# Writing the two parts of each input-projection weight tile to DRAM once and reading them back for three later chunks

## The chip, the cores and the metric

The kernel runs on one core of one Trainium2 chip. The metric is the device time of one launch in microseconds (us). The engines are named as the profile names them: PE is TensorE's matmul, PEld its load of weights, DVE is VectorE, ACT ScalarE, POOL GpSimd, and SP the engine that issues most of the DMAs. Each engine works through its own queue of instructions in a fixed order.

## The reference

One layer of a hybrid decoder over 2048 tokens of width 1024. What matters here is that `h @ w_in` is one projection from 1024 to 3592 columns, over all tokens.

```
h   = rmsnorm(x, norm_mix) * (1.0 + sc_a) + sh_a          # (1, 2048, 1024)
proj = h @ w_in                                           # w_in: (1024, 3592)
sb_q, sb_k, sb_v, dn_qkv, dn_z, dn_a, dn_b = split(proj)  # 512 512 512 1536 512 4 4
o_a = stick_breaking_attention(rmsnorm(sb_q), rmsnorm(sb_k), sb_v)       # 8 heads x 64
q, k, v = split(silu(causal_conv(dn_qkv)))
o_b = rmsnorm(chunk_gated_delta_rule(l2norm(q), l2norm(k), v, g, beta)) * silu(dn_z)   # 4 x 128
x = x + g_a * (concat[o_a, o_b] @ w_out)
h = rmsnorm(x, norm_mlp) * (1.0 + sc_m) + sh_m
x = x + g_m * (square(relu(h @ w_ff1)) @ w_ff2)           # 1024 -> 4096 -> 1024
```

All data are f32. `sc_a`, `sh_a`, `g_a` and the three of the second half come from `silu(c) @ w_ada`.

## The kernel before

**Tiling.** The sequence is cut in four chunks of 512 tokens, which are projected in the order c = 3, 2, 1, 0. For each chunk `project` multiplies all of `w_in` with the chunk's normed activations: 24 blocks of 128 columns (k, v, q of the delta heads, then K, Q of the attention, V, and z) and a small block for the gates. So every weight is used four times, once in each chunk, and each time it is loaded from DRAM anew.

**Two parts.** A product of f32 matrices is made of three products of a shorter type, F32R: the weight tile `ws` is split into `wh`, the value rounded to F32R, and `wl`, the rest; the activations are split in the same way. TensorE adds `wh·ah`, `wh·al` and `wl·ah` (L192 to L194 in `dense`, L212 to L215 in `dense_tok`, L359 to L361 in `wide`).

**One weight unit.** `wunit` makes one pair: the load of `ws` on SP's queue (L171, 128x512 f32, 262144 bytes), the rounding on ScalarE (L172), the subtraction (L173). Of five subtractions in a row two go to GpSimd and three to VectorE. `ws`, `wh` and `wl` each have three buffers in the pool `wp`. A load into `ws` so waits for the cast and the subtraction three units earlier, and the cast for the matmuls that read the `wh` three units earlier: a load can stand six units ahead of the matmuls. A chunk has 56 units: 48 in `dense` (24 blocks, two halves of the depth each; in chunk 3 the first ten of them in `wide`, some with buffers borrowed from other tags) and 8 in `dense_tok` (V). In all there are 224.

**The rest of the mixer.** Between a chunk's projection matmuls, TensorE also does the attention (`attention`, lines L477 to L524) and the delta rule of the chunk before, in two halves of its heads (`delta_half`): pg (the product of the keys), vt and qt (transposes), M and X (a solve by steps on VectorE, L765 and L768, 58 steps for one half), paq, a recurrence, and an output norm whose result goes to DRAM (`mix_d`) and comes back as `mx` and `hm` for the output projection (`outs`, tiles mmo, weights who and wlo, also from `wunit`). The output projection of chunk 3 runs in chunk 1's turn, those of 2, 1 and 0 at the end. Each chunk has a branch (`attention_far`, L540 to L593), which every engine passes and whose body is skipped in this run: work whose instructions stand behind it can't start ahead of it. In chunk 2's turn 32 tiles of `w_ada` of 512 KB are loaded on SP's queue as well (L963, two buffers). After the mixer comes the feed-forward, which the change leaves as it is.

**The order.** The order of each engine's queue is set when the kernel is built, by a scheduler that plays through the program with estimated times and priorities. An edit in one place can so move instructions elsewhere.

Of the kernel before, what the change touches and what calls it, by code (L numbers as in the profile page):

```python
# [7 lines left out]
F32 = mybir.dt.float32  # L8
F32R = mybir.dt.float32r
# [7 lines left out]
P = 128  # L17
# [3 lines left out]
CH = 512  # L21
NCH = SEQ // CH
# [34 lines left out]
def tile_hybrid_layer(  # L57
# [17 lines left out]
    nc = tc.nc  # L75
    V, G, A, T = nc.vector, nc.gpsimd, nc.scalar, nc.tensor

    cp = ctx.enter_context(tc.tile_pool(name="cp", bufs=1))
    dr = ctx.enter_context(tc.tile_pool(name="dr", bufs=1, space=DRAM))

    mx, pms, inner, right = [ctx.enter_context(ExitStack()) for _ in range(4)]
    wp = mx.enter_context(tc.tile_pool(name="wp", bufs=3))
# [49 lines left out]
    if True:  # L132
# [28 lines left out]
        nw = [0]  # L161

        def wunit(src, name, shape=(P, 512), after=None, spots=(None,) * 3):

            ws, wh, wl = [(spot[0] if spot else wp).tile(list(shape), F32 if n == "ws" else F32R, name=n + name,
                                                         tag=spot[1] if spot else n, bufs=spot[2] if spot else 3)
                          for n, spot in zip(("ws", "wh", "wl"), spots)]
            nw[0] += 1
            with tc.high_priority():
                with tc.issue_after(after) if after is not None else nullcontext():  # L170
                    nc.sync.dma_start(ws, src)  # L171
                A.copy(wh, ws)  # L172
                (G if nw[0] % 5 < 2 else V).tensor_tensor(wl, ws, wh.bitcast(F32), ALU.subtract)  # L173
            return wh, wl

        late = []

        def run_late():
# [2 lines left out]
            for f in todo:  # L181
                f()

        def dense(acts, w, evac, name, m0=0):

            for m in range(m0, 4):
                ps = pm.tile([P, CH], F32, tag="mm", name=f"mm{name}_{m}")
                for k in range(KT):
                    if k % 4 == 0:
                        wh, wl = wunit(w[m, :, k:k + 4, :], f"{name}_{m}{k}", (P, 4, P))  # L190
                    ah, al = acts[k]
                    T.matmul(ps, lhsT=wh[:, k % 4, :], rhs=ah, start=k == 0, stop=False)  # L192
                    T.matmul(ps, lhsT=wh[:, k % 4, :], rhs=al, start=False, stop=False)
                    T.matmul(ps, lhsT=wl[:, k % 4, :], rhs=ah, start=False, stop=k == KT - 1)  # L194
                run_late()
                with tc.high_priority():
                    evac(m, ps)

        def dense_tok(acts, w, dst, name):

            for f in range(2):
                if f:
                    run_late()
                ps = [pm.tile([P, 2, 256], F32, tag="mm", name=f"mm{name}_{f}{i}") for i in range(2)]
                for k in range(KT):
                    if k % 2 == 0:
                        src = w[f, :, k:k + 2, :]
                        wh, wl = wunit(src, f"{name}_{f}{k}", (P, 2, 256))
                    ah, al = acts[k]
                    for m in range(4):  # L210
                        o, t = ps[m // 2][:, m % 2, :], slice(m * P, (m + 1) * P)
                        T.matmul(o, lhsT=ah[:, t], rhs=wh[:, k % 2, :], start=k == 0 and m % 2 == 0, stop=False,  # L212
                                 skip_group_check=True)
                        T.matmul(o, lhsT=ah[:, t], rhs=wl[:, k % 2, :], start=False, stop=False, skip_group_check=True)
                        T.matmul(o, lhsT=al[:, t], rhs=wh[:, k % 2, :], start=False, stop=k == KT - 1,  # L215
                                 skip_group_check=True)
                with tc.high_priority():
                    for i in range(2):
                        e = ev.tile([P, 2, 256], F32, tag="ev", name=f"ev{name}_{f}{i}", bufs=3)
                        A.copy(e, ps[i])  # L220
                        nc.scalar.dma_start(dst.rearrange("(m p) f -> p m f", p=P)[:, 2 * i:2 * i + 2,
                                          f * 256:(f + 1) * 256], e)
# [86 lines left out]
        def project(c, acts):  # L309
# [32 lines left out]
            def wide(acts):  # L342

                ps = [pm.tile([P, CH], F32, tag="mm", name=f"mmk{c}_{m}") for m in range(3)]
                ps += [bank(f"mmk{c}_3", [P, CH], "a"), bank(f"mmv{c}_0", [P, CH], "a")]
                spots = {(3, 0): ((at, "ald", 2), (at, "sp", 2), (at, "sp", 2)),
                         (4, 0): ((at, "ald", 2), (at, "aT0", 1), (at, "aT1", 1)),
                         (0, 4): (None, (dn, "ktok0", 1), (dn, "ktok1", 1)),
                         (1, 4): (None, (dn, "dd0", 1), (dn, "dd1", 1)),
                         (2, 4): (None, (dn, "wq0", 1), (at, "qf", 2)),  # L350
                         (3, 4): ((at, "rkb", 1), (at, "av", 2), (at, "av", 2)),
                         (4, 4): ((at, "sn", 1), (at, "om", 1), (at, "qf", 2))}
                for k0 in (0, 4):
                    ws = [wunit(w_m[12 + m, :, k0:k0 + 4, :], f"{'k' if m < 4 else 'v'}{c}_{m % 4}{k0}", (P, 4, P),
                                gate[f"dma{8 + k0}"], spots.get((m, k0), (None,) * 3)) for m in range(5)]
                    for k in range(k0, k0 + 4):
                        ah, al = acts[k]
                        for p, (wh, wl) in zip(ps, ws):
                            T.matmul(p, lhsT=wh[:, k - k0, :], rhs=ah, start=k == 0, stop=False)  # L359
                            T.matmul(p, lhsT=wh[:, k - k0, :], rhs=al, start=False, stop=False)  # L360
                            gate["pe"] = T.matmul(p, lhsT=wl[:, k - k0, :], rhs=ah, start=False, stop=k == KT - 1).ins  # L361
                with tc.high_priority():
                    for m, p in enumerate(ps):
                        conv_out(0 if m < 4 else 8)(m % 4, p)
# [35 lines left out]
            if c == NCH - 1:  # L400
                wide(acts)
            else:
                dense(acts, w_m[12:16], conv_out(0), f"k{c}")
            rs = norm_stats(c - 1) if c > 0 else None
            psab = pm.tile([64, CH], F32, tag="mm", name=f"psab{c}")
            for k in range(KT):
# [14 lines left out]
                    V.tensor_copy(abT[c], pt)  # L421
            late.append(ab_out)

            dense(acts, w_m[16:20], conv_out(8), f"v{c}", 1 if c == NCH - 1 else 0)
            dense(acts, w_m[8:12], conv_out(4), f"q{c}")
            dense(acts, w_m[4:8], head_out(kf_d, 1), f"K{c}")
            dense(acts, w_m[0:4], head_out(qf_d, 0), f"Q{c}")
            late.append(head_rstd)
            dense_tok(acts, w_v, v_d[c], f"V{c}")
            run_late()  # L430
            dense(acts, w_m[20:24], z_out, f"z{c}")
            return rs


# [546 lines left out]
        acts = []  # L981
# [317 lines left out]
```

## Time and profile before

| | us |
|---|---|
| median of 3 runs | 2868.04 |
| lowest and highest run | 2867.67, 2877.46 |
| the profiled execution | 2871.72 |
| its span in the trace | 2869.9 |
| PE busy in it | 2644.2 |
| DVE, ACT, POOL busy in it | 1874.9, 1241.4, 761.6 |

The profile is one execution of the program; the times of its instructions add up to its own time, which lies 3.68 us above the median. The span is the time from the first to the last instruction in the trace. "Busy" of an engine is the time in which it has an instruction under way. The granted clock is the part of TensorE's full clock (2.4 GHz) that it was given; between 1.2 and 2.4 GHz it changes by stages, and a mean of 0.91 is a mixture of the two.

In time, the projection of chunk 3 takes about 39 to 265 us, chunk 2's turn about 265 to 575, chunk 1's 575 to 870, the output projection of chunk 3 870 to 935, chunk 0's turn 935 to 1225, the rest of the mixer to 1510, and the feed-forward to the end.

### The profile page before, as it was taken

How to read it: one execution, taken by the hardware profiler on the slowest of the kernel's cores; microseconds unless marked ns; L12 is line 12 of the kernel's file. 1: busy time of each engine (PE TensorE's matmuls, PEld its weight loads, DVE VectorE, ACT ScalarE, POOL GpSimd, SP SyncE). 2: the span in 40 equal slices, each digit the busy share in tenths (PEclk: the TensorE clock that was granted, in tenths of full speed). 3: DMA queues.
4: the chain of work that ended last, by engine and by line, in shares of the span. 5: the costliest groups of instructions: out<-in, count | busy, mean ns of one | idle time of the engine just before them, and what ended most of it. 6: DMA issues, size and time to landing. Idle time of an engine off the chain costs nothing. (4 is left out here: it accounts for less than half of the span.)

```text
span 2869.9 us, 37558 instructions
## 1 busy us (share of the span) xinstructions
PE 2644.2 (92%) x13044; PEld 2139.5 (75%) x13044; DVE 1874.9 (65%) x4391; ACT 1241.4 (43%) x2421; POOL 761.6 (27%) x592
## 2 busy tenths in 40 slices
PE   3997789889989999899768999999998999999999
PEld 2786568767877778777646888888876888888887
DVE  7665994688748794757765655556568556555655
ACT  4553454355525464354344433343345443344332
POOL 4222311232123221213253222222235222222221
PEclk9999979999989999999989999999999999999999
DMA  7453764443436434463343111111125111111012
GB/s 249 143 165 111 227 218 151 130 139 98 147 109 204 133 120 127 131 203 126 103 137 120 59 55 34 59 59 41 48 88 176 59 59 40 50 59 59 30 59 88
DMA packets 178769, 316.79 MB, mean 110 GB/s; under 512 B 17464, under 2 KB 64504, under 8 KB 174456
## 3 DMA queue, kind: packets, MB, share of 16 engines
q1 hardware_dynamic: 168440, 299.43, 32.2%
q10 hardware_dynamic: 10112, 14.68, 1.4%
q8 instruction: 110, 1.80, 0.3%
q14 instruction: 107, 0.88, 0.1%
HBM read 258.90 MB, written 55.15 MB: 109 GB/s over the span
## 5 line engine op out<-in xcount | busy, mean ns | idle before, releaser
L1190 DVE SCALAR_TENSOR_TENSOR y<-f,mods,y 128x512 f32<-128x512 f32 x512 | 363.6, 746 | 248.2 <-PE f L1187 248.0
L1185 PE MATMUL f<-hidh,wh 128*128 128x512 f32 x1024 | 399.7, 392 | 6.4 <-DVE y L1190 6.2
L1186 PE MATMUL f<-hidl,wh 128*128 128x512 f32 x1024 | 400.4, 391 | 3.2 <-POOL hidl L1168 3.2
L1187 PE MATMUL f<-hidh,wl 128*128 128x512 f32 x1024 | 380.1, 390 | 0.8 <-POOL wl L173 0.8
L1126 PE MATMUL f<-bh,swh 128*128 128x512 f32 x896 | 355.3, 397 | 18.1 <-ACT swh L1119 18.1
L1127 PE MATMUL f<-bl,swh 128*128 128x512 f32 x896 | 354.1, 395 | 0.0
L1128 PE MATMUL f<-bh,swl 128*128 128x512 f32 x896 | 348.5, 396 | 0.7 <-DVE swl L1120 0.6
L1185 PEld LDWEIGHTS f<-hidh,wh 128*128 128x128 f32 x1024 | 192.6, 188 | 53.2 <-DVE y L1190 10.8
L1186 PEld LDWEIGHTS f<-hidl,wh 128*128 128x128 f32 x1024 | 192.7, 188 | 44.6 <-POOL hidl L1168 4.3
L1187 PEld LDWEIGHTS f<-hidh,wl 128*128 128x128 f32 x1024 | 192.6, 188 | 42.5 <-POOL wl L173 1.2
L1126 PEld LDWEIGHTS f<-bh,swh 128*128 128x128 f32 x896 | 168.4, 188 | 61.0 <-ACT swh L1119 20.4
L172 ACT CAST wh<-ws 128x512 fp32r<-128x512 f32 x128 | 79.5, 621 | 299.9 <-PE f L1186 243.6
L1128 PEld LDWEIGHTS f<-bh,swl 128*128 128x128 f32 x896 | 168.1, 188 | 43.8 <-DVE swl L1120 2.8
L1127 PEld LDWEIGHTS f<-bl,swh 128*128 128x128 f32 x896 | 168.4, 188 | 40.9 <-issue 0.2
L1168 POOL TENSOR_TENSOR hidl<-t,hidh 128x512 fp32r<-128x512 f32 x64 | 102.1, 1595 | 335.0 <-ACT hidh L1167 315.4
L1119 ACT CAST swh<-wa 128x512 fp32r<-128x512 f32 x96 | 59.4, 622 | 265.5 <-PE f L1127 259.2
L1112 POOL TENSOR_TENSOR sws<-wa 128x512 f32<-128x512 f32 x64 | 88.9, 1389 | 309.6 <-DVE wl L173 284.8
L1140 DVE TENSOR_TENSOR t<-t,f 128x512 f32<-128x512 f32 x128 | 87.3, 683 | 121.0 <-PE f L1128 87.3
L1120 DVE TENSOR_TENSOR swl<-sws,swh 128x512 fp32r<-128x512 f32 x128 | 143.1, 1118 | 22.2 <-ACT swh L1119 22.2
L1120 DVE TENSOR_TENSOR swl<-wa,swh 128x512 fp32r<-128x512 f32 x96 | 86.8, 907 | 100.2 <-ACT swh L1119 100.2
L173 POOL TENSOR_TENSOR wl<-ws,wh 128x512 fp32r<-128x512 f32 x52 | 68.1, 1311 | 247.5 <-ACT wh L172 247.0
L1141 ACT ACTIVATE t<-t 128x512 f32<-128x512 f32 x128 | 80.8, 632 | 86.2 <-DVE t L1140 86.2
(353 smaller groups left out, 6193.0 us busy)
## 6 DMA issues: line engine op xcount, KB each, us to landing
wa<-in_w_ff_dram SPq DMA_DIRECT2D x32, 1024.0 KB
ws<-in_w_ff_dram SPq DMA_DIRECT2D x128, 256.0 KB
wada<-in_w_ada_dram SPq DMA_DIRECT2D x48, 512.0 KB
wso<-in_w_out_dram SPq DMA_DIRECT2D x64, 256.0 KB
cv_d<-ev SPq DMA_DIRECT2D x48, 256.0 KB
cv<-cv_d SPq DMA_DIRECT2D x24, 512.0 KB
x<-in_xc_dram SPq DMA_DIRECT2D x40, 256.0 KB
wsk<-in_w_m_dram SPq DMA_DIRECT2D x32, 256.0 KB
```

The source lines that it names most:

```text
L1112: G.tensor_tensor(t, x, y, op)
L1120: V.tensor_tensor(wl, x, wh.bitcast(F32), SUB)
L1126: T.matmul(ps, lhsT=wh[:, k, :], rhs=ah, start=first and k == 0, stop=False, skip_group_check=True)
L1127: T.matmul(ps, lhsT=wh[:, k, :], rhs=al, start=False, stop=False, skip_group_check=True)
L1128: T.matmul(ps, lhsT=wl[:, k, :], rhs=ah, start=False, stop=stop and k == 3, skip_group_check=True)
L1140: V.tensor_tensor(t, t, ps, op)
L1141: A.activation(t, t, AF.Relu)
L1168: (G if i % 2 else V).tensor_tensor(hl, x, hh.bitcast(F32), SUB)
L1185: T.matmul(ps[n], lhsT=wh[:, s], rhs=ah, start=j == 0, stop=False)
L1186: T.matmul(ps[n], lhsT=wh[:, s], rhs=al, start=False, stop=False)
L1187: T.matmul(ps[n], lhsT=wl[:, s], rhs=ah, start=False, stop=j == 1)
L1190: V.scalar_tensor_tensor(ys[m][:, cs], ps[n], mods[:, 40 + m:41 + m], ys[m][:, cs], ALU.mult, ALU.add)
```

## The change

A new function `wparts` takes the place of `wunit` for the 56 units of the input projection. For chunk 3, which is projected first, it calls `wunit` as before and then writes `wh` (on ScalarE's queue) and `wl` (on SP's queue) to DRAM tiles, 112 writes of 262144 bytes. For the chunks 2, 1 and 0 there is no load of `ws`, no cast and no subtraction: `wh` and `wl` are loaded, both on SP's queue, 336 loads where 168 were. For every third unit the two tiles take the buffers of the tag `ws`, so that the buffers of all three tags stay in use. The output projection and the feed-forward still use `wunit`, whose counter `nw` goes on counting.

```
...
+        wm_d = [[dr.tile([2, P, CH], F32, name=f"wm_d{m}_{k}") for k in range(2)] for m in range(24)]
+        wv_d = [[dr.tile([2, P, CH], F32, name=f"wv_d{f}_{k}") for k in range(4)] for f in range(2)]
+
+        def wparts(c, src, dst, name, shape, after=None, spots=(None,) * 3):
+            if c < NCH - 1:
+
+                nw[0] += 1
+                ws = [wp.tile(list(shape), F32R, name=n + name, tag="ws" if nw[0] % 3 == 0 else n, bufs=3)
+                      for n in ("wh", "wl")]
+                with tc.high_priority():
+                    for i, t in enumerate(ws):
+                        nc.sync.dma_start(t.bitcast(F32), dst[i].rearrange("p (a b) -> p a b", a=shape[1]))
+                return ws
+            ws = wunit(src, name, shape, after, spots)
+            for i, t in enumerate(ws):
+                (nc.sync if i else nc.scalar).dma_start(dst[i].rearrange("p (a b) -> p a b", a=shape[1]), t.bitcast(F32))
+            return ws
...
-                        wh, wl = wunit(w[m, :, k:k + 4, :], f"{name}_{m}{k}", (P, 4, P))
+                        src, shape = w[m, :, k:k + 4, :], (P, 4, P)
+                        if parts is None:
+                            wh, wl = wunit(src, f"{name}_{m}{k}", shape)
+                        else:
+                            c, m_in = parts
+                            wh, wl = wparts(c, src, wm_d[m_in + m][k // 4], f"{name}_{m}{k}", shape)
...
-                        wh, wl = wunit(src, f"{name}_{f}{k}", (P, 2, 256))
+                        wh, wl = wparts(c, src, wv_d[f][k // 2], f"{name}_{f}{k}", (P, 2, 256))
...
-                    ws = [wunit(w_m[12 + m, :, k0:k0 + 4, :], f"{'k' if m < 4 else 'v'}{c}_{m % 4}{k0}", (P, 4, P),
+                    ws = [wparts(c, w_m[12 + m, :, k0:k0 + 4, :], wm_d[12 + m][k0 // 4],
+                                 f"{'k' if m < 4 else 'v'}{c}_{m % 4}{k0}", (P, 4, P),
...
```

The other lines of the diff hand `(c, m_in)` or `c` to `dense` and `dense_tok`. In the code after, the loads are line L188, the writes L192; the casts and subtractions keep L172 and L173, and later lines move down by 24 or 25.

**Where the order moves.** On SP in the projection of chunk 3, at the loads for the q blocks (`ws`, L171) and the columns that go to DRAM for the convolution (`cv_d`), the order of before is:

```order
L171 DMA wsq3_00_842<-in_w_m_dram 128x512
L333 DMA cv_d3_102<-ev3_8_619 128x512
L171 DMA wsq3_04_860<-in_w_m_dram 128x512
L333 DMA cv_d3_102<-ev3_9_737 128x512
L171 DMA wsq3_10_888<-in_w_m_dram 128x512
L171 DMA wsq3_14_906<-in_w_m_dram 128x512
L171 DMA wsq3_20_934<-in_w_m_dram 128x512
L333 DMA cv_d3_102<-ev3_10_786 128x512
L171 DMA wsq3_24_952<-in_w_m_dram 128x512
```

The order of after at the same place, with the writes to wm_d (L192):

```order
L171 DMA wsq3_10_980<-in_w_m_dram 128x512
L192 DMA wm_d19_1_189<-wlv3_34_902 128x512
L171 DMA wsq3_14_1000<-in_w_m_dram 128x512
L192 DMA wm_d8_0_166<-wlq3_00_932 128x512
L171 DMA wsq3_20_1030<-in_w_m_dram 128x512
L192 DMA wm_d8_1_167<-wlq3_04_952 128x512
L357 DMA cv_d3_102<-ev3_10_870 128x512
L171 DMA wsq3_24_1050<-in_w_m_dram 128x512
L192 DMA wm_d9_0_168<-wlq3_10_982 128x512
L171 DMA wsq3_30_1080<-in_w_m_dram 128x512
L192 DMA wm_d9_1_169<-wlq3_14_1002 128x512
```

Each load of a `ws` is now followed by the write of a `wl` of a unit four or so earlier.

On SP in chunk 2's turn, at the loads for the v and q blocks among those of `w_ada` (wada), before:

```order
L333 DMA cv_d2_101<-ev2_3_4072 128x512
L171 DMA wsv2_30_4299<-in_w_m_dram 128x512
L689 DMA cv2_1_0_5483<-cv_d2_101 128x4x256
L963 DMA wada25_9419<-in_w_ada_dram 128x1024
L171 DMA wsv2_34_4317<-in_w_m_dram 128x512
L963 DMA wada26_9423<-in_w_ada_dram 128x1024
L171 DMA wsq2_00_4346<-in_w_m_dram 128x512
L963 DMA wada27_9427<-in_w_ada_dram 128x1024
L459 DMA akf3_3_3349<-kf_d3_90 128x512
```

And after:

```order
L988 DMA wada24_9471<-in_w_ada_dram 128x1024
L188 DMA whv2_24_4412<-wm_d18_1_187 128x512
L188 DMA wlv2_24_4413<-wm_d18_1_187 128x512
L714 DMA cv2_1_0_5539<-cv_d2_101 128x4x256
L988 DMA wada25_9475<-in_w_ada_dram 128x1024
L188 DMA wlv2_20_4397<-wm_d18_0_186 128x512
L188 DMA whv2_34_4455<-wm_d19_1_189 128x512
L988 DMA wada26_9479<-in_w_ada_dram 128x1024
L988 DMA wada27_9483<-in_w_ada_dram 128x1024
L188 DMA whv2_30_4439<-wm_d19_0_188 128x512
L188 DMA wlv2_30_4440<-wm_d19_0_188 128x512
```

A unit's one load became two, `wh` and `wl`; of a unit in the tag `ws` (here v2_20) the second load stands apart from the first, behind loads of later units.

On PE at the last branch, that of chunk 0: pg is the product of the keys of half 0 of the delta heads, mmo1 the output projection of chunk 1. Before, the first rows behind the branch (the jump is its end) are:

```order
L542 UNCONDITIONAL_BRANCH x2
L192 MATMUL mmo1_0_3_27694<-hm1_1_27522,who1_0_30_27696 128x512
L193 MATMUL mmo1_0_3_27694<-lm1_1_27523,who1_0_30_27696 128x512
L194 MATMUL mmo1_0_3_27694<-hm1_1_27522,wlo1_0_30_27697 128x512
L192 MATMUL mmo1_0_3_27694<-hm1_2_27528,who1_0_30_27696 128x512
L731 MATMUL pg0_0_1_19551<-cv0_0_0_19497 128x128 x4
L193 MATMUL mmo1_0_3_27694<-lm1_2_27529,who1_0_30_27696 128x512
```

After, ahead of the branch, between the attention's matmuls of chunk 0 (z, pa):

```order
L756 MATMUL pg0_0_0_19396<-cv0_0_0_19329 128x128 x4
L502 MATMUL z0_3_11_20244<-maskr_145,identr_144 128x2x128
L509 MATMUL z0_3_11_20244<-akf0_3_20181,qf0_3_20188 128x256 x2
L260 MATMUL ss22_27190<-idon_69,acc22_26836 128x1 x4
L720 MATMUL vt0_0_1_19415<-idon_69,cv0_0_8_19409 128x128 x4
L720 MATMUL vt0_0_0_19421<-idon_69,cv0_0_8_19409 128x128 x4
L538 MATMUL pa0_3_1_0_20267<-idon_69,sp0_3_1_20242 128x128 x4
L538 MATMUL pa0_3_1_1_20274<-idon_69,sp0_3_1_20242 128x128 x4
L720 MATMUL qt0_0_1_19569<-idon_69,cv0_0_4_19562 128x128 x4
```

The products pg and the transposes vt and qt of half 0 moved from behind the last branch to ahead of it. On VectorE 16 of the 58 steps X of this half moved ahead of it with them (none stood there before), and on PE 54 matmuls of mmo1 moved from ahead of the branch to behind it: 171 stand there after, 117 before.

## Rows read from the trace of the kernel before

**Rows 1.** The page's parts 1 and 5: PE over the span, one feed-forward matmul group.

```profile
PE 2644.2 (92%) x13044; PEld 2139.5 (75%) x13044; DVE 1874.9 (65%) x4391; ACT 1241.4 (43%) x2421; POOL 761.6 (27%) x592
...
L1185 PE MATMUL f<-hidh,wh 128*128 128x512 f32 x1024 | 399.7, 392 | 6.4 <-DVE y L1190 6.2
```

**Rows 2.** Stretches: bounds, length, busy PE, PEld, DVE, ACT, POOL (instructions), clock, DMA, GB/s.

```profile
39.00:265.00 226.00, 198.25 (x1086) 165.95 (x1086) 145.43 (x455) 106.04 (x210) 57.27 (x50) 0.95 0.47 154
265.00:575.00 310.00, 270.19 (x1449) 216.79 (x1448) 239.63 (x781) 141.87 (x311) 75.66 (x64) 0.91 0.56 179
575.00:870.00 295.00, 268.41 (x1585) 221.13 (x1584) 207.77 (x661) 139.59 (x317) 64.66 (x61) 0.94 0.40 125
935.00:1225.00 290.00, 271.84 (x1576) 221.90 (x1576) 210.69 (x685) 143.03 (x325) 59.96 (x54) 0.95 0.42 128
...
1510.00:2870.00 1360.00, 1338.56 (x5770) 1081.56 (x5770) 801.47 (x1055) 530.71 (x892) 375.01 (x263) 0.99 0.19 65
```

**Rows 3.** PE's waits, 265 to 1225 us: total, times, longest.

```profile
PE pa L513 <- DVE nt L125: 11.1, 1, 11.1
...
PE mmz L192 <- ACT whz L172: 1.1, 1, 1.1
```

**Rows 4.** Stretch view, the middle of chunk 2's turn, columns as in rows 2.

```profile
300.00:450.00 150.00, 122.58 (x541) 92.38 (x540) 143.60 (x468) 78.03 (x164) 24.91 (x19) 0.85 0.68 221
```

**Rows 5.** Stretch view of line L173 alone: bounds, length, busy DVE, POOL, clock, DMA.

```profile
265.00:575.00 310.00, 25.73 (x36) 32.92 (x23) 0.91 0.56 179
575.00:870.00 295.00, 23.44 (x33) 29.00 (x22) 0.94 0.40 125
935.00:1225.00 290.00, 24.04 (x34) 29.79 (x23) 0.95 0.42 128
300.00:450.00 150.00, 11.68 (x16) 15.92 (x10) 0.85 0.68 221
```

**Rows 6.** DVE's timeline: start, length, instruction.

```profile
308.24 1.52 DVE L173 TENSOR_TENSOR wlk<-wsk,whk 128x512 fp32r<-128x512 f32 x1
...
322.48 0.69 DVE L173 TENSOR_TENSOR wlv<-wsv,whv 128x512 fp32r<-128x512 f32 x1
```

**Rows 7.** Line L173, 265 to 1225 us: shortest, median, longest ns, first and last start.

```profile
L173 DVE TENSOR_TENSOR wlk<-wsk,whk x15: 676/683/1518, 266.4 to 977.4; 128x512 fp32r<-128x512 f32 x15
...
L173 DVE TENSOR_TENSOR wlq<-wsq,whq x14: 646/681/693, 385.0 to 1057.7; 128x512 fp32r<-128x512 f32 x14
...
L173 POOL TENSOR_TENSOR wlq<-wsq,whq x10: 1270/1291/2257, 393.0 to 1046.7; 128x512 fp32r<-128x512 f32 x10
```

**Rows 8.** Stretch view of single slices, columns as in rows 2.

```profile
10.00:20.00 10.00, 1.70 (x8) 1.71 (x8) 7.63 (x16) 6.43 (x11) 0.18 (x1) 1.00 1.01 362
320.00:330.00 10.00, 9.26 (x48) 6.16 (x45) 10.00 (x33) 5.91 (x18) 0.00 (x0) 1.00 0.90 299
```

**Rows 9.** Timelines of the queues of SP and ACT: DMA issues.

```profile
325.25 11.68 SPq L963 DMA_DIRECT2D wada<-in_w_ada_dram  x4
...
145.69 0.34 ACTq L373 DMA_DIRECT2D kf_d<-ev  x1
```

**Rows 10.** ACT's timeline: casts after a late load, idle time and its end in brackets.

```profile
161.65 0.62 ACT L172 CAST whQ<-wsQ 128x512 fp32r<-128x512 f32 x1 [4.71 <-DMA wsQ<-in_w_m_dram]
...
555.43 0.62 ACT L172 CAST whz<-wsz 128x512 fp32r<-128x512 f32 x1 [9.85 <-DMA wsz<-in_w_m_dram]
```

**Rows 11.** Stretch view, from the last branch to the last mix, columns as in rows 2.

```profile
1350.00:1454.00 104.00, 75.18 (x437) 61.33 (x436) 73.35 (x287) 29.67 (x72) 29.94 (x26) 0.88 0.33 104
```

**Rows 12.** DVE's timeline behind the last branch.

```profile
1353.74 0.69 DVE L871 TENSOR_REDUCE so<-sqo 128x4 f32<-128x512 f32 x1 [3.84 <-ACT who L172]
...
1369.48 1.25 DVE L751 STREAM_TRANSPOSE M<-Gt 128x1024 f32<-128x1024 f32 x1 [0.94 <-POOL Gt L737]
```

**Rows 13.** Line L768, 1350 to 1510 us, the solve's steps.

```profile
L768 DVE TENSOR_TENSOR X<-X,tm x58: 157/183/1328, 1372.1 to 1405.0; 128x24 f32<-128x24 f32 x6, 128x27 f32<-128x27 f32 x4, 128x30 f32<-128x30 f32 x4, 128x26 f32<-128x26 f32 x3
```

**Rows 14.** ACT's timeline at the end of the mixer.

```profile
1452.01 1.89 ACT L892 CAST hm<-mx 128x512 fp32r<-128x512 f32 x3 [10.34 <-DMA mx<-mix_d]
```

More of the change, by code (lines that the diff above doesn't have):

```diff
@@ L182, in run_late, with dense @@
                 f()
-        def dense(acts, w, evac, name, m0=0):
+        def dense(acts, w, evac, name, m0=0, parts=None):
             for m in range(m0, 4):
@@ L197, in dense, with dense_tok @@
                     evac(m, ps)
-        def dense_tok(acts, w, dst, name):
+        def dense_tok(acts, w, dst, name, c):
             for f in range(2):
@@ L402, in project @@
             else:
-                dense(acts, w_m[12:16], conv_out(0), f"k{c}")
+                dense(acts, w_m[12:16], conv_out(0), f"k{c}", 0, (c, 12))
             rs = norm_stats(c - 1) if c > 0 else None
@@ L422, in project @@
             late.append(ab_out)
[L424 to L427, printed above, removed]
+            dense(acts, w_m[16:20], conv_out(8), f"v{c}", 1 if c == NCH - 1 else 0, (c, 16))
+            dense(acts, w_m[8:12], conv_out(4), f"q{c}", 0, (c, 8))
+            dense(acts, w_m[4:8], head_out(kf_d, 1), f"K{c}", 0, (c, 4))
+            dense(acts, w_m[0:4], head_out(qf_d, 0), f"Q{c}", 0, (c, 0))
             late.append(head_rstd)
-            dense_tok(acts, w_v, v_d[c], f"V{c}")
+            dense_tok(acts, w_v, v_d[c], f"V{c}", c)
             run_late()
-            dense(acts, w_m[20:24], z_out, f"z{c}")
+            dense(acts, w_m[20:24], z_out, f"z{c}", 0, (c, 20))
             return rs
```

## The prediction

> **What bounds the kernel now.** I read the page first: TensorE is busy in 2644.2 us of a span of 2869.9 [rows 1]. An edit that takes work from VectorE, ScalarE and GpSimd can therefore gain only where TensorE is idle or slow, and the table by stretches says where that is [rows 2]. In the feed-forward (1510 to 2870) TensorE is busy 1338.56 of 1360 us at a granted clock of 0.99, and the change does not touch it. The three stretches in which chunks 2, 1 and 0 are projected hold the work that goes away. There TensorE is idle 310 − 270.19 = 39.8, 295 − 268.41 = 26.6 and 290 − 271.84 = 18.2 us, and the granted clock is 0.91, 0.94 and 0.95. At 1.2 in place of 2.4 GHz the shortfall is worth (1 − 0.91) × 310 = 28, 18 and 14.5 us. So TensorE loses about 68, 44 and 33 us, 145 in all, and this is the most that the three reloads can give back.
>
> Next, whether TensorE waits for the weights. In its waits from 265 to 1225 us the longest single one (11.1 us) is for a VectorE step of the norm's statistics (nt), and of the weights whz is named, with 1.1 us [rows 3]. Weights are made well ahead of need. What is left of the gain is indirect: VectorE, relieved of subtractions, is earlier with what TensorE does wait for. The place is 300 to 450 us, where VectorE is busy 143.60 of 150 us and TensorE 122.58, at a clock of 0.85 [rows 4].
>
> **Chunk 2: −20 us.** In the stretch of this chunk the subtractions hold VectorE 25.73 us (36 of them), 11.68 of these between 300 and 450 [rows 5]. There VectorE is full, so I count all of that as path: −12. GpSimd makes 10 more in the same time, and they slow VectorE: a VectorE subtraction beside one lasts 1.52 us, another alone 0.69 [rows 6]. Ten times the 0.83 between them is 8 us at most; half of these on the path gives −4. With TensorE idle for shorter the clock should fall less often; of the 22.5 us that (1 − 0.85) × 150 makes I take a sixth, −4. Ends: 0, if VectorE's freed time is filled with other queued work that nobody waits for; −68, all of TensorE's loss there. ScalarE's casts go too, but ScalarE is busy 141.87 of 310 us [rows 2] and I count them at nothing.
>
> How much GpSimd's subtractions cost VectorE has a second reading. The VectorE groups have medians of 683 and 681 ns, with a few up to 1518, and GpSimd's last 1.29 us [rows 7]; so most met no neighbour. The Trainium skill (SBUF — State Buffer, Who interferes with whom) says that a VectorE instruction with two SBUF inputs contends with a GpSimd instruction that reads SBUF, and that of two on the shared port pair one blocks fully. The slow subtraction agrees; by that rule every VectorE instruction with two inputs could lose as much, and the term would be nearer −8 than −4.
>
> **Chunks 1 and 0: −10 us.** VectorE is busy 70% and 73% of these stretches [rows 2] and the subtractions are 23.44 and 24.04 us of it [rows 5]. An engine with a quarter of its time free gives back only the pieces on which somebody waits: I take a fifth, 5 us each. Ends: 0 and −77 (44 + 33).
>
> **Chunk 3 and its writes: +7 us.** 56 units × 2 parts × 262144 bytes = 29.4 MB are written in the 226 us of that stretch, which moves 154 GB/s × 226 us = 34.8 MB now, at a share of 0.47 [rows 2]. The sum is 284 GB/s, and the share 0.47 × 64.2 / 34.8 = 0.87 on the mean. The most that any 10 us show is 362 GB/s at 1.01 [rows 8], so the writes fit, but not in every piece: the first of them fall in slices already full. On SP, wl's write of a unit now stands between the loads of later units; it waits there for its subtraction, and the next loads behind it wait too, as do those of w_ada in the start-up. On ScalarE 56 issues of about 0.34 us [rows 9] are 19 us beside 106 busy of 226 [rows 2]: hidden. I take +7, a late load or two. Ends: 0 and 29.4 MB / 362 GB/s = +81, nothing hidden. The Trainium skill (DMA: Bandwidth & Descriptors, Issuing engines are not separate DMA queues) says that DMAs issued from ScalarE and SP run on the same 16 engines and interleave, which speaks against a gain from sending wh and wl by different queues; the trace of before, which has no such pair of writes, does not show it. By that rule the term could only be nearer its upper end.
>
> **New waits for the loads: +10 us.** Each of 168 units now loads 0.52 MB in place of 0.26: 14.7 MB more per chunk. In chunk 2 that makes 179 × 310 / 1000 + 14.7 = 70.2 MB, 226 GB/s at a share of 0.71; between 300 and 450 (221 GB/s, 0.68 [rows 4], 16 + 10 units [rows 5]) it makes 266 GB/s and 0.82. In single slices there is no room: 320 to 330 is at 0.90 already [rows 8]. SP's queue is in order and stalls: four loads of w_ada took it 11.68 us [rows 9], and the order of after puts the weights' loads, two for a unit, among those of w_ada. Before, a load stood six units ahead of TensorE's use. After, every third unit takes both its tiles from the three of one tag, so its second load waits until TensorE is through with the unit three before it. A unit that comes late costs what stands for the two late loads of before: ScalarE sat 4.71 and 9.85 us for wsQ and wsz [rows 10], though TensorE, with finished units in hand, lost 1.1 [rows 3]. That cushion of finished units is thinner now. I take two late loads at 4.7 us. Ends: 0 and one unit in ten, 17 × 4.7 = +80.
>
> **The tail of the mixer: −20 us.** The work of half 0 of chunk 0 (pg, vt, qt, and the solve on VectorE) all stood behind the last branch, and the order of after brings pg, vt, qt and 16 of the 58 X steps ahead of it, putting more of chunk 1's output projection behind it. Now TensorE is busy 75.18 of 104 us from 1350 to 1454 at 0.88 [rows 11]. Behind the branch come a row sum at 1353.74 and the solve's M at 1369.48 [rows 12], X from 1372.1 to 1405.0 [rows 13], and the cast of hm at 1452.01, which waits for the last mix [rows 14]: 98 us. Taken ahead are 17 us up to X and 16/58 of the 33 us of X, 9: a chain of 98 − 26 = 72 us. TensorE's own work there grows by the 54 matmuls that the order moves behind the branch, 54 × 0.392 [rows 1] = 21 us, to 96, less some 5 for pg, vt and qt. TensorE, not the chain, is then the longer, 91 against 104 with the idle before; and what it no longer does ahead of the branch may bring that forward by part of 21 us. −20; ends 0 (the branch comes later by what was moved ahead of it) and −37, TensorE's idle 28.8 and 8 of clock.
>
> **Sum.** +7 − 20 − 10 + 10 − 20 = −33: 2871.72 − 33 = 2838.7 for the profiled execution. The median of the runs, 2868.04, is 3.7 lower, so 2835.
>
> **Rivals.** *More relief.* Half of TensorE's 145 us comes back instead of 30: VectorE's lateness and the low clock feed each other at 300 to 450 us. For it speaks the clock of 0.85 there; against it, that the long waits are for chains and not for subtractions. 2835 − 43 = 2792.
>
> *Nothing moves.* VectorE's freed time lies beside TensorE's work, the tail's branch comes later by what was brought ahead of it, and +7 and +10 stand against some −20: 2855 to 2862. For it speaks that TensorE was waiting for weights only 1.1 us.
>
> *Late loads, slower.* In chunks 2 to 0 the loads are issued behind w_ada's and behind the tile that TensorE still holds, and TensorE waits itself. Without a late load the sum is −43: at 4.7 us each, nine late units use that up, twelve make the kernel slower by 14, and one unit in ten (17) gives −43 + 80: 2868 + 37 = 2905. It decides from nine late units on. For it: SP's 11.68 us stall and slices of 0.90; against: means of 0.71 and, in chunks 1 and 0, 0.40 × 51.6 / 36.9 = 0.56.
>
> *Writes not hidden, slower.* Chunk 3 grows by the 81 us of its upper end in place of 7, with SP's loads held behind the writes: 2835 + 74 = 2909; from 40 us on it takes up the gain. For it speaks a share of 0.87 on the mean.
>
> *The change does not do what it says.* The diff and the order of after show no cast and no subtraction for chunks 2 to 0 and 336 loads, so I give this no chance.
>
> **How the numbers follow.** About 0.5% (14.3 us) is what a measurement of this kernel can tell from no change. Forecast 0.48, more relief 0.10: faster by over 0.5%, 0.58. Nothing moves 0.21: same. Late loads 0.14, writes not hidden 0.07: slower, 0.21. The range runs from 2790, the larger relief, to 2895, within the slower cases: of their 0.21 about 0.14 lies beyond, and about 0.05 below 2790.
>
> **What would show it.** Right: from 300 to 450 us VectorE below 135 of 150 and TensorE above 130; chunk 3's stretch longer by under 10 us with a DMA share near 0.87; TensorE's waits for wh or wl of under 15 us in all; from the branch to the cast of hm about 80 us in place of 98. Wrong: rows of TensorE that wait for a DMA of wh or wl again and again (late loads); chunk 3 longer by tens of us (writes); or the three stretches as long as before with VectorE merely idler.

## The result

Over five runs of each the kernel before has a median of 2874.39 us (2867.67 to 2878.4) and the changed one 2850.80 (2845.64 to 2856.13). The ratio is 0.9918, with a 95% interval of 0.9899 to 0.9936: 23.6 us faster (18 to 29). The forecast was 33 us faster: 2835 us, counted from the 2868.04 of three runs, while the median of before over five runs lies 6 us higher. The profiled execution of the changed kernel took 2854.6 us, its span is 2852.8, 17.1 shorter than that of before.

The page's first part, of the changed kernel (compare the first line with [rows 1]):

```profile
PE 2631.5 (92%) x13044; PEld 2135.1 (75%) x13044; DVE 1775.0 (62%) x4290; ACT 1165.0 (41%) x2263; POOL 659.5 (23%) x525
```

VectorE lost 100 us of work, ScalarE 76, GpSimd 102, and the kernel 17 to 24. The stretch view with the bounds of [rows 2], and the last line that of [rows 4], in the same columns:

```profile
39.00:265.00 226.00, 194.88 (x1070) 162.72 (x1069) 143.98 (x455) 104.59 (x209) 55.25 (x49) 0.95 0.77 264
265.00:575.00 310.00, 270.76 (x1482) 218.80 (x1480) 214.05 (x784) 115.25 (x261) 44.67 (x44) 0.91 0.73 237
575.00:870.00 295.00, 271.51 (x1628) 224.37 (x1626) 188.88 (x709) 121.38 (x285) 36.18 (x40) 0.95 0.56 174
935.00:1225.00 290.00, 263.18 (x1575) 213.64 (x1574) 177.23 (x677) 121.54 (x281) 21.06 (x28) 0.95 0.56 173
...
300.00:450.00 150.00, 126.02 (x610) 95.79 (x609) 134.65 (x477) 70.17 (x152) 10.46 (x12) 0.88 0.84 283
```

The DMA shares of the chunks that read back are near those worked out ahead: 0.73 in chunk 2 (0.71 forecast) and 0.56 in chunks 1 and 0. In chunk 3 the share is 0.77 and not 0.87: 264 GB/s over 226 us are 59.7 MB, and 64.2 had been counted. In the last line VectorE is free for 15 us instead of 6, and TensorE busy for 126.02 instead of 122.58 at a clock of 0.88 instead of 0.85.

Where the 17 us of the profiled execution lie is read best from the first matmul of each chunk. Chunk 2's stands at 273.26 us before and at 276.60 in the changed kernel. TensorE's timeline of before, the first matmuls of chunks 1 and 0:

```profile
573.85 0.50 PE L192 MATMUL mmk<-h,whk 128*128 128x512 f32 x1
934.80 0.50 PE L192 MATMUL mmk<-h,whk 128*128 128x512 f32 x1
```

And of the changed kernel:

```profile
572.98 0.50 PE L216 MATMUL mmk<-h,whk 128*128 128x512 f32 x1
929.41 0.48 PE L216 MATMUL mmk<-h,whk 128*128 128x512 f32 x1
```

The feed-forward starts at 1513.49 us before and at 1496.89 in the changed kernel. Chunk 3 is 3.3 us longer, chunk 2's turn 4.2 shorter (296.4 for 300.6), chunk 1's 4.5 and chunk 0's with the tail 11.2; the feed-forward is the same to half a us. Each of these is read from a single execution, and the scheduler moves matmuls from one turn to another (chunk 1's turn holds 1929 of them before and 1983 after), so a few us in one turn say little. From chunk 2's first matmul to the feed-forward the work is the same, 6137 matmuls. The stretch view of that, before and then changed, columns as in [rows 2]:

```profile
273.26:1513.49 1240.23, 1094.70 (x6137) 882.70 (x6135) 899.71 (x2818) 584.53 (x1285) 311.86 (x262) 0.93 0.47 148
276.60:1496.89 1220.29, 1080.42 (x6136) 874.85 (x6135) 802.19 (x2716) 508.55 (x1129) 212.26 (x195) 0.93 0.59 186
```

Of the 20 us that it is shorter, TensorE's busy time gave 14 and its idle time 6.

A new wait came. TensorE's waits from 265 to 1225 us in the changed kernel (total, times, longest; compare [rows 3]):

```profile
PE mmz L218 <- DMA wlz<-wm_d: 18.7, 4, 7.6
...
PE mmk L218 <- DMA wlk<-wm_d: 7.0, 2, 3.8
```

Before, TensorE waited for no load of a weight itself (once, 1.1 us, for the cast behind a late one, [rows 3]); now it does six times in these two groups, 25.7 us in all, and once more for 0.4 us, each time for a `wl`.

### The profile page after: what moved, and what is told of

Read it like the earlier page. It is cut to its first block, busy times and chain, and to the rows that moved or that the text cites. A ratio compares the mean times of both kernels' runs of the same rounds, so it can differ in the third digit from the quotient of the medians.

```text
span 2852.8 us, 37490 instructions
## 1 busy us (share of the span) xinstructions
PE 2631.5 (92%) x13044; PEld 2135.1 (75%) x13044; DVE 1775.0 (62%) x4290; ACT 1165.0 (41%) x2263; POOL 659.5 (23%) x525
## 4 chain that ended last, share of the span: by engine, by line
PE 47%; DVE 2%; DMA 2%; issue 1%; POOL 1%; ACT 0%; SPq 0%; DVEq 0%; POOLq 0%; ACTq 0%
PE f L1210 8%; PE f L1211 8%; PE f L1212 8%; PE f L1151 7%; PE f L1152 7%; PE f L1153 7%; DMA fx<-x_d 1%; DVE fx L1067 0%; DVE bl L130 0%; PE mmo L216 0%; PE mmo L218 0%; PE mmo L217 0%; DVE y L1215 0%; DMA mx<-mix_d 0%; DMA rs_d<-acc 0%
## 5 line engine op out<-in xcount | busy, mean ns | idle before, releaser
L172 ACT CAST wh<-ws 128x512 fp32r<-128x512 f32 x128 | 79.5, 621 | 301.1 <-PE f L1211 245.6
L173 POOL TENSOR_TENSOR wl<-ws,wh 128x512 fp32r<-128x512 f32 x52 | 67.6, 1301 | 248.8 <-ACT wh L172 248.4
```

## Experiments

All ratios are to runs of the kernel before on the same chip, about 2875 us, so 0.001 is 2.9 us.

**Half of the change alone: the writes (e1).** Chunks 2 to 0 call `wunit` as before.

```
             if c < NCH - 1:
...
-                return ws
+                return wunit(src, name, shape)
```

> Chunk 3 writes both parts as in the changed kernel, but chunks 2, 1 and 0 load, cast and subtract as before; what is read back is nothing. Prices the writes and the order that comes with them. My theory (writes cost the 3 us by which the end of chunk 3's z matmuls moved in the changed kernel; the gain lies in the relief of chunks 2 to 0 and behind the last branch): end of chunk 3's z 2 to 6 us later than before, the whole kernel at 0.997 to 1.002 of before; anything under 1 would come from the order behind the last branch, where pg of half 0 stands ahead of the branch here too. Rival (writes are a hidden cost of the changed kernel that it pays in other places as well): above 1.004.

Measured: 1.0003 (0.9988 to 1.0017). The 29.4 MB of writes cost 0.9 us, −3.4 to +4.9. Chunk 2's first matmul stands at 276.9 us in its trace, 3.6 later than before. At the last branch this kernel has the matmuls of mmo1 where the changed one has them (only 20 ahead of it) and part of pg ahead, but vt, qt and all 58 steps X behind it as before.

**The other half, without the second load (e2).** wh alone is written, read back, and used twice.

```
             if c < NCH - 1:
...
+                t = wp.tile(list(shape), F32R, name="wh" + name, tag=("wh", "wl", "ws")[nw[0] % 3], bufs=3)
+                with tc.high_priority():
+                    nc.sync.dma_start(t.bitcast(F32), dst[0].rearrange("p (a b) -> p a b", a=shape[1]))
+                return t, t
```

> Chunk 3 writes wh alone (56 writes); chunks 2, 1 and 0 read wh back and use it in the place of wl as well, so the small part of the weights is left out of the sums there. No cast, no subtraction, one load for a unit as before, six units of buffers or more. Shows what the relief gives without the second load. My theory (late second loads cost the changed kernel some 26 us of TensorE's waits): no wait of TensorE for a weight over 1 us, and 0.983 of before, 49 us. Rival (late loads are slack that other waits would take): 0.992, as the changed kernel.

Measured: 0.9816 (0.9796 to 0.9836), 53 us faster; TensorE waits for no weight. The stretch from 300 to 450 us of this kernel, and the same length 12 us earlier:

```profile
300.00:450.00 150.00, 131.21 (x674) 99.53 (x673) 120.93 (x448) 61.54 (x142) 3.35 (x5) 0.91 0.66 215
288.00:438.00 150.00, 125.12 (x615) 95.29 (x615) 131.81 (x476) 64.28 (x147) 11.81 (x12) 0.90 0.70 229
```

The first line looks like the picture that the prediction drew of chunk 2: VectorE has 29 us to spare, TensorE is busy 131.21 us, the clock is at 0.91. But chunk 2 starts 12 us earlier here (261.5 us for 273.3), so the same bounds hold a later piece of it. The second line has the piece that [rows 4] show of before: TensorE 125.12 us for 122.58, at 0.90 for 0.85. And 12 of the 53 us were gained in chunk 3, from which no subtraction was taken; the relief is not 53 us (see e5).

**The subtractions alone (e12).** Nothing written or read back; loads and casts as before, but `wh` takes turns in the tags of `wh` and `wl` and so has six buffers for three.

```
             if c < NCH - 1:
...
+                with tc.high_priority():
+                    nc.sync.dma_start(ws, src)
+                    A.copy(wh, ws)
+                return wh, wh
```

> The kernel before with 168 subtractions left out: in chunks 2, 1 and 0 each weight tile is loaded once and cast once, as before, and wh is used in the place of wl, so the small part of the weights is left out of the sums there. Nothing is written to DRAM or read back. With the run that reads wh back alone (0.9816: no cast, no subtraction, and six more tiles in the pool's turn) it divides the relief. My theory (the prediction's: the subtractions on VectorE and GpSimd carry the relief, the casts nothing): 0.982 to 0.986. Rival (the casts, in ScalarE's queue between the loads and the matmuls, carry half of it or more): 0.990 to 0.995.

Measured: 0.9849 (0.9829 to 0.9870), 43 us. Leaving out the subtractions is enough for this, as the prediction had it; what of it the three further buffers gave is not shown. The 10 us between this and e2 (the intervals overlap) are about the 12 by which e2's chunk 3 is shorter. But the gain does not lie where the prediction put it. The stretch from 300 to 450 us of e12:

```profile
300.00:450.00 150.00, 122.06 (x565) 91.53 (x565) 133.50 (x474) 80.47 (x169) 10.12 (x11) 0.85 0.70 229
```

VectorE is relieved of 10 us there, and TensorE is busy 122.06 us at 0.85: as before (122.58 at 0.85).

**Do the late `wl` make the second load dear? (e3)** In the changed kernel each third unit takes both its tiles from one tag of three buffers. Here the tiles rotate.

```
-                ws = [wp.tile(list(shape), F32R, name=n + name, tag="ws" if nw[0] % 3 == 0 else n, bufs=3)
-                      for n in ("wh", "wl")]
+                ws = [wp.tile(list(shape), F32R, name=n + name, tag=g, bufs=3)
+                      for n, g in zip(("wh", "wl"), (("wh", "wl"), ("ws", "wh"), ("wl", "ws"))[nw[0] % 3])]
```

> The changed kernel with one edit: the two tiles of a unit in chunks 2 to 0 take turns through the three tags (wh and wl, then ws and wh, then wl and ws), so that no unit takes two buffers of one tag; bytes, loads and queue as in the changed kernel. My theory (late loads come of the unit that takes both tiles from one tag): TensorE's waits for DMA of wl fall from 26 us to under 8, and the kernel goes to 0.985 of before. Rival (late loads come of SP's queue or of full DMA engines): 20 to 30 us of such waits stay and the time is 0.992 again.

Measured: 0.9922 (0.9904 to 0.9940), the same as the changed kernel. TensorE's waits of this kernel, 265 to 1225 us:

```profile
PE mmz L218 <- DMA wlz<-wm_d: 9.5, 4, 3.1
...
PE mmk L216 <- DVE ev L356: 6.0, 2, 4.2
```

So most of the late loads came of the shared tag (they fell from 26.1 to 9.5 us), and the time did not move. Most of the 17 us came back as other waits: that of mmk for ev (6.0) is not in the list of the changed kernel at all, and all of TensorE's waits in this stretch add up to 85 us here and 90 there. A wait for a late weight was no price by itself.

**Which half of the extra traffic costs (e5, e6).** e5 writes both parts and reads wh alone; e6 writes wh alone and loads it twice.

> Chunk 3 writes wh and wl (112 writes, as in the changed kernel); chunks 2, 1 and 0 read back wh alone and use it in the place of wl too, so the small part of the weights is left out of the sums there. With the run that writes and reads wh alone (0.9816) and the rotated full reload (0.9922) it divides the 30 us between them. My theory (the second load of each unit is the price): 0.981 to 0.985. Rival (the writes of wl on SP in chunk 3, with the order that they bring, are the price; chunk 3 ended 12 us earlier without them): 0.988 to 0.992, with chunk 3's z ending 2 to 6 us later than before.

Measured: 0.9853 (0.9828 to 0.9877).

> The other half: chunk 3 writes wh alone (56 writes); chunks 2, 1 and 0 load that wh twice, into two tiles in turn through the three tags, so bytes and loads there are those of the changed kernel, and the small part of the weights is left out of the sums. My theory (second loads are the price): 0.988 to 0.992. Rival (the writes of wl are the price): 0.981 to 0.985.

Measured: 0.9843 (0.9823 to 0.9864). With e2 and e3 this makes a square:

| | one load a unit | two loads a unit |
|---|---|---|
| one write a unit | 0.9816 (e2) | 0.9843 (e6) |
| two writes a unit | 0.9853 (e5) | 0.9922 (e3) |

e5 lies at the edge of its theory (0.985), which makes the second loads the price, and e6 in the range of its rival, which makes the writes the price. Both can't be: added to e2 alone, the second load costs 8 us, which the noise can make, and the second write 11, and both together 30.

The square's first row misleads. Its kernels, e2 and e6, start chunk 2 at 261.5 and 259.6 us; e5 starts it at 274.1, but so do the kernels that write nothing (273.3 before, 272.8 in e12). The 12 us are therefore no price of a second write: the order that came with one write happens to save them. Where they lie shows in TensorE's timelines. Before, and in e5 as well (9.84 us at 245.75), a product of the delta rule ahead of z waits for VectorE; the line is that of before:

```profile
244.44 1.22 PE L853 MATMUL p<-vz,ktok 128*128 128x128 f32 x4 [9.49 <-DVE vz L848]
```

VectorE stands there at a step (akf) that waits for rkb. VectorE's timeline of e5:

```profile
244.49 0.75 DVE L485 SCALAR_TENSOR_TENSOR akf<-akf,gqk,rkb 128x512 f32<-128x512 f32 x1 [7.26 <-DMA rkb<-rk_d]
```

In e2 that step comes 7 us earlier and the same product stands at 240.58 us without a wait. So the square's second row is the one to read, with e12 beside it: without a second load 42 us are gained (e5) and 43 without any reload (e12), and the second load takes 20 of them back (0.9922 against 0.9853, clear of both intervals).

**SP's queue (e7).** The rotated reload with the `wl` loaded from ScalarE's queue.

```
-                        nc.sync.dma_start(t.bitcast(F32), dst[i].rearrange("p (a b) -> p a b", a=shape[1]))
+                        (nc.scalar if i else nc.sync).dma_start(t.bitcast(F32), dst[i].rearrange("p (a b) -> p a b", a=shape[1]))
```

> The rotated full reload with the loads of wl issued by ScalarE and those of wh by SP; bytes, buffers and writes unchanged. If SP's queue (its issues, or its stalls among the loads of w_ada) makes the second load dear, 0.984 to 0.988 of before. If the 16 DMA engines or the buffers do: 0.990 to 0.994; slower still, above 0.994, if ScalarE then waits for buffers ahead of its own work.

Measured: 0.9889 (0.9867 to 0.9911), the fastest of those that leave nothing out, 32 us under before; TensorE waits 2.8 us for loads of weights. Chunk 2's turn lasts 279.6 us (before 300.6, changed 296.4), but chunk 0's with the tail 578.4, as long as before (578.7; e3 563.2). Over chunk 2's own turn the changed kernel moves 233 GB/s at a DMA share of 0.71, e7 244 at 0.74. That is as much in a given busy time, so the second queue brought no transfer rate. This agrees with the Trainium skill (DMA: Bandwidth & Descriptors, Issuing engines are not separate DMA queues), which grants a second issuing engine only the time of the issues. That the shorter turn comes of the queue and not of the order that moved with it is not shown.

**SP without any `wl` (e9), and more buffers (e10).** Both start from e7. e9 moves the writes of `wl` to ScalarE's queue too; e10 adds two tiles to the rotation, 11 in place of 9. The edit of e9, and then that of e10:

```
-                (nc.sync if i else nc.scalar).dma_start(dst[i].rearrange("p (a b) -> p a b", a=shape[1]), t.bitcast(F32))
+                nc.scalar.dma_start(dst[i].rearrange("p (a b) -> p a b", a=shape[1]), t.bitcast(F32))
```

```
+        wx = sb("wx", 2, right, "right")
...
+                    g = ("wh", "wl", "ws", "wx", "wh", "wl", "ws", "wx", "wh", "wl", "ws")[turn[0] % 11]
+                    turn[0] += 1
```

> The rotated reload with ScalarE issuing the loads of wl (0.9889), and now both writes of chunk 3 as well, so that SP's queue carries nothing of wl. If wl's writes in SP's queue hold back the loads behind them in chunk 3: 0.985 to 0.987, chunk 3's z ending before 270 us. If the writes cost nothing, as the run with the writes alone (1.0003) says: 0.988 to 0.990.

Measured: 0.9957 (0.9942 to 0.9971), 20 us slower than e7.

> The rotated reload with ScalarE issuing the loads of wl, and two more tiles: 11 buffers for two tiles a unit, 5.5 units in place of 4.5. If the thinner cushion of buffers makes the second load dear: 0.984 to 0.987. If the DMA engines do, or nothing but the order of the queues: 0.988 to 0.990.

Measured: 0.9928 (0.9913 to 0.9942), 11 us slower than e7, although TensorE waits for no load of a weight. Both missed. One of ScalarE's waits from 39 to 600 us, of e9; evV waits in the same way for 9.3 us:

```profile
ACT qt L729 <- DMA wlv<-wm_d: 11.0, 1, 11.0
```

Neither qt nor evV reads a `wl`. In ScalarE's queue the issue of a `wl` stands right ahead of each (at 333.97 us ahead of qt, at 505.82 of evV), so that what stands behind it is late. e7 has such waits as well (evz 11.1 us behind an issue of a `wlz`, ev 6.0 behind one of a `wlV`), so they do not explain the 20 us by themselves.

**Reload in chunks 1 and 0 only (e8).**

```
+            if c == NCH - 2:
+                return wunit(src, name, shape)
-            if c < NCH - 1:
+            if c < NCH - 2:
```

> The rotated reload in chunks 1 and 0 only; chunk 2, whose turn carries the 32 loads of w_ada, loads, casts and subtracts as before. My theory (chunk 2 gives a third or less of the gain, because its second loads meet a DMA share of 0.72 to 0.84): 0.993 to 0.996. Rival (chunk 2, where VectorE is full, gives most of it): 0.997 to 1.001.

Measured: 0.9981 (0.9969 to 0.9993), 5.5 us. By the number the rival held: without the reload in chunk 2, 17 of e3's 22 us are gone. Its reason is not shown. Chunk 2's turn lasts 306.8 us here and 302.6 in e3, 4 us apart; 18 us lie in chunk 0's turn and the tail (581.7 and 563.2), where the two kernels do the same work.

**The order at the last branch (e4, e11).** e4 is the kernel before with pg, vt, half of qt and paq, 38 steps X and all of mmo1 ahead of the branch; e11 the changed kernel with vt, qt, paq and all 58 steps X behind it. The edit of e4, and then that of e11:

```
-            with tc.high_priority(offset=800 if c == 0 else 1):
+            with tc.high_priority(offset=1):
                 carry = attention(c)
```

```
+            with tc.high_priority(offset=650 if c == 0 else 800):
                 delta_half(c, 0, terms)
```

> The kernel before with one edit: the attention of chunk 0 loses its raised priority, so the scheduler puts the last branch later: pg, vt, qt, paq of half 0, 38 of 58 steps X and all of chunk 1's output projection stand ahead of it. No weight is written or read back. My theory (the 14 us gained behind the last branch are the order's, not the freed VectorE's): 10 to 20 us faster than before, 0.993 to 0.997. Rival (order alone gives nothing, since the branch comes later by what is put ahead of it): 0.999 to 1.003.

Measured: 0.9993 (0.9980 to 1.0006). The stretch view of e4 from its branch to the last cast of hm:

```profile
1387.00:1460.00 73.00, 41.38 (x262) 32.26 (x263) 41.96 (x159) 17.38 (x42) 12.97 (x10) 0.79 0.23 71
```

The branch stands 37 us later than before (1387.3 for 1350.3), and what is left behind it is short but empty: TensorE is busy 41 of 73 us. What was brought ahead of the branch delayed it.

> The changed kernel with a lower priority for half 0 of chunk 0's delta rule: pg stays ahead of the last branch, but vt, qt, paq and all 58 steps X stand behind it again, as before. The prediction's term for the tail (17 us up to X and 9 of X taken out of the chain behind the branch): 10 us or more are lost, 0.995 to 0.998. Rival (what stands ahead of the branch delays the branch, and TensorE's work behind it fills the rest): 0.990 to 0.993, as the changed kernel.

Measured: 0.9913 (0.9898 to 0.9927), as the changed kernel. The rival held.

**All kernels turn by turn.** The lengths in each profiled execution, in us, from the first matmuls of the chunks and of the feed-forward:

| | chunk 3 | chunk 2 | chunk 1 | chunk 0 and tail | chunk 2 to tail |
|---|---|---|---|---|---|
| before | 273.3 | 300.6 | 361.0 | 578.7 | 1240.2 |
| e4 (order alone) | 275.2 | 304.6 | 357.7 | 583.0 | 1245.3 |
| e1 (writes alone) | 276.9 | 307.7 | 365.6 | 571.6 | 1244.9 |
| e12 (no subtraction) | 272.8 | 296.4 | 353.1 | 560.9 | 1210.4 |
| e5 (two writes, one load) | 274.1 | 297.1 | 346.0 | 564.0 | 1207.1 |
| e2 (one write, one load) | 261.5 | 292.9 | 352.0 | 561.3 | 1206.1 |
| e6 (one write, two loads) | 259.6 | 291.3 | 354.1 | 568.7 | 1214.0 |
| changed | 276.6 | 296.4 | 356.4 | 567.5 | 1220.3 |
| e3 (rotated) | 276.4 | 302.6 | 353.9 | 563.2 | 1219.7 |
| e7 (two queues) | 274.9 | 279.6 | 352.9 | 578.4 | 1210.9 |
| e9 (writes of `wl` moved too) | 279.4 | 295.1 | 366.5 | 566.2 | 1227.7 |
| e10 (more buffers) | 271.4 | 298.8 | 356.2 | 569.5 | 1224.5 |
| e11 (solve behind the branch) | 274.7 | 298.1 | 346.0 | 573.1 | 1217.3 |
| e8 (chunks 1 and 0 only) | 275.6 | 306.8 | 353.2 | 581.7 | 1241.8 |

The feed-forward, which no edit touches, takes 1353 to 1358 us in them, so 5 us in one execution are noise. Three kernels without any relief lie at 1240 to 1245 in the last column, three with the relief and no second load at 1206 to 1210, and those that load twice in all three chunks between, at 1211 to 1228.

## Why the prediction came near, point by point

**The relief of chunks 2 to 0, −30 us forecast: about −43 measured (e12; e5 −42).** The subtractions are its carrier, as forecast. Its path was not the one named. Chunk 2 was to give 20 of the 30, because VectorE is full from 300 to 450 us. In the changed kernel VectorE fell there to 134.65 of 150 us (under 135 was asked) and TensorE rose to 126.02 and not above 130; in e12, with VectorE at 133.50, TensorE did not rise at all, and chunk 2's turn is only 4 us shorter. What the prediction counted least gave most in e12: the clock. With (1 − clock) times length, as there, summed over a hundred slices from chunk 2's first matmul to the feed-forward, the shortfall falls from 90 us before to 73 in e12 and 83 in the changed kernel; a sixth of 22.5 us, 4, had been counted. In chunk 1's turn the granted clock is 0.98 in e12 and 0.95 before, with TensorE idle for 20 us in place of 29. Why the relief arrives there and not in chunk 2 stays open.

The reading of GpSimd's part rests on the wrong neighbour. In the trace, what GpSimd ran beside the slow VectorE subtraction at 308.24 us [rows 6] was first an addition of the norm's statistics (L259, 307.95 to 309.21), which the change leaves in place, and a subtraction of its own only from 309.17 on.

**The tail, −20 forecast: its mechanism fell.** In the changed kernel the chain behind the branch was shortened as worked out, and more. The line of the solve's steps (compare [rows 13]):

```profile
L793 DVE TENSOR_TENSOR X<-X,tm x58: 157/180/1311, 1329.9 to 1361.0; 128x24 f32<-128x24 f32 x6, 128x27 f32<-128x27 f32 x4, 128x30 f32<-128x30 f32 x4, 128x26 f32<-128x26 f32 x3
```

The solve ends 44 us earlier, at 1361.0. But hm's cast comes 17 us earlier (compare [rows 14]; ScalarE's timeline):

```profile
1434.98 0.62 ACT L917 CAST hm<-mx 128x512 fp32r<-128x512 f32 x1 [10.45 <-DMA mx<-mix_d]
```

From the branch (1336.3, before 1350.3) that is 98.7 us, before 101.7; the forecast was 80. The chain lost its gain behind the solve. TensorE's timelines have the first of the short products pz and the last of pu there, before and then changed:

```profile
1407.92 0.59 PE L814 MATMUL pz<-xt,mt 32*32 32x32 f32 x16
1415.07 1.06 PE L829 MATMUL pu<-bv,xbd 128*128 128x128 f32 x8
```

```profile
1362.76 0.59 PE L839 MATMUL pz<-xt,mt 32*32 32x32 f32 x16
1390.55 1.06 PE L854 MATMUL pu<-bv,xbd 128*128 128x128 f32 x8
```

These steps take 28 us for 7: 99 matmuls of the output projection now stand between them in TensorE's queue, where none did, and TensorE is busy for all 27.79 us from the first to the last. The branch came 14 us earlier, 5 of them because chunk 0's turn began earlier. e4 and e11 say that such an exchange across the branch is worth nothing. The step that failed is the first of that part, that a shorter chain makes the end earlier; its sentence on TensorE, which "is then the longer", was the right half. Its sum was wrong too: 54 × 0.392 us takes each matmul at its full length, but they overlap. By [rows 2] 5770 of them keep TensorE busy for 1338.56 us, 0.23 each, so the 54 are 12.5 us and not 21.

**The writes, +7, and the late loads, +10: 17 forecast, about 20 measured (the changed kernel and e3 against e12 and e5).** The writes by themselves are the cheaper end (e1: +0.9 us, with the DMA share at 0.77 in the stretch where the forecast had 0.87): the mean share was the right row to lean on, and the bound of +81 was far off. So the second loads cost about 20 and not 10. The late loads were forecast as two of 4.7 us, under 15 us in all; there were seven, up to 7.6 us each, 26.1 us. But the reason was wrong too. I priced a load by how late its matmul is, and e3, e7 and e10 took most or all of that lateness away (9.5, 2.8 and 0 us) at 0.9922, 0.9889 and 0.9928. Neither tag nor buffers nor the issues on SP alone are the price.

What it is stays open. Six kernels with the same bytes, the same matmuls and the full reload (the changed one, e3, e7, e9, e10, e11) lie at 0.9918, 0.9922, 0.9889, 0.9957, 0.9928 and 0.9913: 20 us apart by edits of a line or two that move instructions in all queues. So the price of the second loads lies anywhere from 10 to 30 us, by the order that they come with. The 12 us of chunk 3 in e5 and e2 show one case of what an order does, where a step that waits for a small load stands ahead of the delta rule's on VectorE. That more DMAs in the queues make more such places is argued, not shown.

**The sum.** The relief was worth 13 us more than forecast, the tail's exchange nothing in place of 20, and the traffic 3 more than 17: −33 became −23. That the forecast came so near is in part luck, since the first two of these misses have opposite signs. Each kernel here is one order of the queues, and six with the same work lie 20 us apart, so the single terms are no surer than that.

**The rivals.** *More relief* (2792 us) did not come even where nothing is loaded twice: e2 is at 2823 and e12 at 2834. Its thought that the clock would give back more was right in kind: 17 us in e12. *Nothing moves* and both slower ones fell: chunk 3 grew by 3.3 us, not 74, and the late loads, which came more often than forecast, hit a kernel that had other waits in their place.

## What to carry to other kernels

Leave the work out first: a run without the 168 subtractions (43 us) tells about what avoiding them can bring, before one pays for writes and loads. Of a shorter chain ask what stands between its next steps in the queue of the busiest engine; here a solve that ended 30 us sooner behind the branch gave 3. Compare a stretch with the same work, not with the same clock time: 12 us of shift made e2's chunk 2 look far better than it is. And where a scheduler sets the order, judge an edit by several siblings: here six of them scattered over 20 us, nearly as much as the edit is worth.

## What was not expected of the hardware

Writes and reads together filled the DMA engines in chunk 3, and TensorE lost nothing by it in that slice. The stretch view of the changed kernel:

```profile
160.00:170.00 10.00, 10.00 (x57) 8.60 (x57) 5.53 (x15) 3.64 (x7) 6.08 (x9) 1.00 1.02 366
```

Before, the same slice moved 167 GB/s at a share of 0.47, with TensorE as busy (10.00 us, 55 matmuls). From 300 to 450 us e7 held 291 GB/s at 0.86 with TensorE busier (135.48 of 150 us) than in any other run of that stretch. A DMA share of 0.86 over 150 us, or of 1.02 over 10, did not slow TensorE by itself. The fullest 10 us of before are not those of [rows 8]: from 1510 to 1520 us it moves 372 GB/s at 1.03.
